# Attention scores one step later in three head groups, probabilities turned in one step and weighed in the next, the last weight block in two column halves, lambda's operations fourteen steps later

## The chip, the cores and the metric

The kernel runs on one core of one Trainium2 chip. The metric is the device time of one execution in microseconds (us). The profiled execution gives, beside its own time, a span: the stretch from the first to the last recorded instruction, which is what all positions below are counted in. A core has a matrix engine (TensorE, PE in the profile, with PEld for its weight loads), a vector engine (DVE), a scalar engine (ACT), a general engine (POOL) and a sync engine (SP) that here only issues transfers. Each engine works through its own list of instructions in order, and engines wait for one another by semaphores. SP, ACT and POOL can issue transfers (DMA) from their lists.

## The reference

Two layers over a sequence of 256 rows of width 2048, all in float32. Layer 0 mixes with a state-space scan, layer 1 with differential attention, and each is followed by a SwiGLU network of width 5632. Every part is normed before and after:

```python
for i in range(DEPTH):                       # DEPTH = 2
    h = rmsnorm(x, norm_mix_pre[i])
    m = ssd_mixer(h, ...) if i % 2 == 0 else diff_attention(h, ...)
    x = x + rmsnorm(m, norm_mix_post[i])
    h = rmsnorm(x, norm_ffn_pre[i])
    x = x + rmsnorm(swiglu(h, ...), norm_ffn_post[i])

def diff_attention(...):                     # 16 heads, 2 maps of width 64, v of width 128
    lam = exp(sum(lq1 * lk1)) - exp(sum(lq2 * lk2)) + lambda_init
    # per block of 128 queries, causal:
    pr = softmax(s)                          # s: scores of both maps
    pr = pr[:, :, 0] - lam * pr[:, :, 1]
    o = pr @ v                               # per head
    o = rmsnorm(o, subln_w) * (1 - lambda_init)
    return o @ w_out
```

## The kernel before, in words

**Products.** The matrix engine keeps float32 accuracy by splitting each operand in a high and a low part: ACT casts the high part `hi` (L137), DVE subtracts to get the low part `lo` (L138), and a product is three matmuls, hi by hi, hi by lo and lo by hi. Weights come in blocks of 1 MB, sent by SP's queue into three raw buffers; each block is split in two passes of 128x2048 and used by halves. The 256 rows of x are two tiles, `t` = 0 and 1. `mv` (L181) holds x as the stationary operand and streams 512 columns of weights: for each half block it runs the six matmuls of t = 0 at once and puts those of t = 1 on a list that is worked off a few halves later. When a tile's last half is through, it calls `evac` for the accumulated tile `acc`, which lies in one of four PSUM buffers. `ws` does the q and k products of the attention, with the weights stationary (L239, L241) and four column tiles `acc[0..3]`, which need all four PSUM buffers.

**What sets the order.** Small work is not written where it is needed but handed to `later(k, fn)`, which runs `fn` k steps on; a step (`tick`) is one half block of `mv` or `ws`, 12 matmuls of 512 columns in `mv`. The order of the code so made is then passed through a scheduler that sets the final order on each engine, so the code alone doesn't say what stands beside what.

**Attention.** `attention_group(hg)` handles four heads; there are four groups. It runs `mv` for v, `ws` for q and `ws` for k, and hands on, for the steps of the next group's `mv` and `ws`: `all_scores` (the scores of query tile 1 head pair 0, tile 0, tile 1 head pair 1, L1055, then the softmax operations on DVE and ACT), `turn` (transposes of the probabilities on the matrix engine, L1091, and their copy by ACT, L1093), `weigh` (probabilities by v, L1102, then a norm per head: square on ACT L1106, sums on DVE L1108 and L1109, a power on POOL L1111, a product on DVE L1112 into `ob`), and `piece` (transposes of `ob`, L326, for the output projection). The keys are scaled by `rstd_bc` on DVE (L1038) behind the addition L1035 that evacuates them; the scores wait for that. For the last group the steps are those of the output projection.

**Lambda.** `lamv`, a row of 256 numbers repeated over 128 partitions (128 KB on chip), is fetched by a DMA that ACT issues (L997). DVE multiplies and sums (L1000, L1001), ACT takes the exponent (L1002, with a load of its function table), DVE subtracts (L1004, L1005) into `neglam`, which the softmax uses. All this is written between the FFN of layer 0 and the first group. Between the two also lie the norms that end the FFN (`norm_chain`: x updated on DVE, L682, transposed on the matrix engine, L688 `ptx`, split into `xT`, L693 and L694).

**End.** `out_proj` accumulates the last FFN's output in four column blocks n of 512. On n = 3 the evacuation of each tile adds to `m` (L780), squares and sums on ACT (L337), multiplies by the norm's weights (L719, `mw`), and calls `norm_chain`, which here has `final` set: `rs_post` by L94 on DVE and L97 on POOL, then for n = 0 a scaling on ACT (L679) and an addition on POOL (L680), for n = 1 to 3 one operation on DVE (L682), and for each n a DMA of 256 KB to the output, all issued by SP (L684).

Of the kernel before, what the change touches and what calls it, by code (L numbers as in the profile page):

```python
# [45 lines left out]
def trunk_kernel(ctx, tc, x_rows, x_cols, vec_cols, vec64, post_rows, lam_rows,  # L46
# [134 lines left out]
    def mv(blocks, stat, evac, lag, scale=None, loaded=()):  # L181
# [3 lines left out]
        def run(i, t, hi, lo):  # L185
            if i == 0:
                acc[t] = accp.tile([P, 512], F32, tag="acc", name="acc")
            for j in range(2):
                xh, xl = stat(i, j, t)
                for q, (a, b) in enumerate(((xh, hi), (xh, lo), (xl, hi))):  # L190
                    nc.tensor.matmul(acc[t], a, b[:, j], start=(i == 0 and j == 0 and q == 0),  # L191
                                     stop=(i == last and j == 1 and q == 2))
            if i == last:
                evac(t, acc[t])
# [477 lines left out]
    def norm_chain(t, ss4, last_mw, step, final, t512):  # L672

        rn = rstd_of(ss4[:, 3:4], D, f"post{step}_{t}", ss4[:, 0:1])
        for n in range(4):
            mw = last_mw if n == 3 else m[(t, n)]
            xt = xres[(t, n)]
            if final and n == 0:
                nc.scalar.activation(mw, mw, AF.Copy, scale=rn)  # L679
                nc.gpsimd.tensor_tensor(xt, xt, mw, op=ALU.add)  # L680
            else:
                nc.vector.scalar_tensor_tensor(xt, mw, rn, xt, op0=ALU.mult, op1=ALU.add)  # L682
            if final:
                nc.sync.dma_start(out[t * P:(t + 1) * P, n * 512:(n + 1) * 512], xt)  # L684
                continue
# [23 lines left out]
    def out_proj(w, first, last, acts, kgs, step, final, lag, t512, pw, scale=None, ns=range(4), two={}, forms=None, md=None, mid=None,  # L709
# [56 lines left out]
        for n in ns:  # L766
# [7 lines left out]
            def evac(t, ps, n=n):  # L774
# [19 lines left out]
            if weave and n < 2:  # L794
# [5 lines left out]
               (lambda i: [scale[:, 2 * up[i] + j:2 * up[i] + j + 1] for j in range(2)]) if scale is not None else None)  # L800
# [195 lines left out]
    lamv = t512("lamv", (P, 4, 64))  # L996
    nc.scalar.dma_start(lamv, lam_rows.partition_broadcast(P))  # L997
    lsum = const.tile([P, 2], F32, name="lsum")
    for e in range(2):
        nc.vector.tensor_tensor(lamv[:, 2 * e], lamv[:, 2 * e], lamv[:, 2 * e + 1], op=ALU.mult)  # L1000
        nc.vector.tensor_reduce(lsum[:, e:e + 1], lamv[:, 2 * e], axis=AX.X, op=ALU.add)  # L1001
    nc.scalar.activation(lsum, lsum, AF.Exp)  # L1002
    neglam = const.tile([P, 1], F32, name="neglam")
    nc.vector.tensor_tensor(neglam, lsum[:, 1:2], lsum[:, 0:1], op=ALU.subtract)  # L1004
    nc.vector.tensor_scalar(neglam, neglam, -LAMBDA_INIT, None, op0=ALU.add)  # L1005
# [6 lines left out]
    def attention_group(hg):  # L1012
# [112 lines left out]
        later(2, all_scores)  # L1125
        later(6, lambda: turn(0, (0, 1)))
        later(8, lambda: (turn(1, (0,)), weigh(0)))
        later(10, lambda: turn(1, (1,)))
# [68 lines left out]
```

## Time and profile before

| what | value |
| --- | --- |
| median of three runs | 2509.29 us (2508.55, 2509.29, 2509.58) |
| profiled execution, its own time | 2509.47 us |
| span of that execution | 2507.6 us |
| granted clock of TensorE, mean | 0.999 |
| bytes moved | 541 MB, mean 216 GB/s |

The profiled execution lies 0.18 us above the median, and its span leaves 1.9 us of its time outside. A matmul's row gives its start and its length to the end of its drain; matmuls overlap, so that what one costs is the distance to the next one's start. In a row of the timeline the first number is the start, the second the length of the whole group, "x4" the number of instructions in it, and the bracket at the end says how long the engine was idle before and what released it.

### The profile page before, as it was taken

To read this page: it belongs to the slowest core of one execution; us is meant where nothing else is said; L and a number is where in the kernel's file an instruction comes from. 1 tells how busy PE (TensorE), PEld (TensorE's weight loads), DVE (VectorE), ACT (ScalarE), POOL (GpSimd) and SP (SyncE) were. 2 spreads that over 40 slices of the span, in tenths; PEclk is the share of its full clock that TensorE was granted. 3 is DMA by queue.
4 is the path that set the end of the run, shared out by engine and by line. 5 is a ranking of instruction groups with operands and counts; after the bars stand their busy time and mean duration, and the time that the engine had idled before them with its cause. 6 is when DMAs were issued, how large, how long until landed. Compare 5 with 4: busy or idle time off the path is not lost.

```text
span 2507.6 us, 31493 instructions
## 1 busy us (share of the span) xinstructions
PE 2489.6 (99%) x11818; PEld 2062.5 (82%) x11818; DVE 1936.8 (77%) x2394; ACT 1403.2 (56%) x1895; POOL 263.8 (11%) x242
## 2 busy tenths in 40 slices
PE   9999999999999999999999999999999999999998
PEld 8888888888888888888888888888888888888886
DVE  6877547777688899978987766556688899879985
ACT  5767546665565455545554654455655465546553
POOL 0131000121110010001001100001100100020002
PEclk9999999999999999999999999999999999999999
DMA  7555555555786786868676544544776967686774
GB/s 287 195 171 199 185 191 195 175 179 192 255 275 202 253 256 215 256 209 265 217 247 237 185 171 144 199 167 143 255 234 207 289 223 232 217 265 225 224 247 151
DMA packets 143385, 541.43 MB, mean 216 GB/s; under 512 B 14400, under 2 KB 31104, under 8 KB 116224
## 3 DMA queue, kind: packets, MB, share of 16 engines
q1 hardware_dynamic: 125872, 503.96, 57.7%
q0 software_dynamic: 16992, 35.13, 7.1%
q8 instruction: 93, 1.52, 0.2%
q14 instruction: 60, 0.49, 0.1%
q10 hardware_dynamic: 368, 0.32, 0.1%
HBM read 520.41 MB, written 18.94 MB: 215 GB/s over the span
## 4 chain that ended last, share of the span: by engine, by line
PE 93%; DVE 2%; issue 1%; ACT 1%; DMA 1%; POOL 0%; SPq 0%; DVEq 0%; ACTq 0%; POOLq 0%
PE acc L265 38%; PE acc L191 33%; PE cp L265 9%; PE acc L239 5%; PE acc L241 2%; PE acc L216 2%; DVE lo L138 1%; PE pt_f L326 1%; ACT hi L137 1%; DMA raw<-in_w_g_dram 1%; PE py L607 1%; PE ptx L688 0%; PE po L1102 0%; PE pc L509 0%; PE px L594 0%
## 5 line engine op out<-in xcount | busy, mean ns | idle before, releaser
L138 DVE TENSOR_TENSOR lo<-raw,hi 128x2048 fp32r<-128x2048 f32 (+2 forms) x401 | 728.8, 1821 | 307.8 <-ACT hi L137 300.9
L137 ACT CAST hi<-raw 128x2048 fp32r<-128x2048 f32 (+2 forms) x401 | 604.6, 1511 | 432.9 <-PE acc L191 122.7
L191 PE MATMUL acc<-hi,xT 128*128 128x512 f32 x1792 | 570.3, 394 | 0.0
L265 PE MATMUL acc<-hi,xT 128*128 128x512 f32 x1608 | 518.7, 390 | 0.1
L191 PEld LDWEIGHTS acc<-hi,xT 128*128 128x128 f32 x1792 | 336.0, 188 | 71.4 <-issue 2.2
L265 PEld LDWEIGHTS acc<-hi,xT 128*128 128x128 f32 x1608 | 301.8, 188 | 63.0 <-DVE sx L748 0.5
L191 PE MATMUL acc<-lo,xT 128*128 128x512 f32 x896 | 351.9, 393 | 1.4 <-DVE lo L138 1.4
L265 PE MATMUL acc<-lo,xT 128*128 128x512 f32 x804 | 313.0, 389 | 0.0
L138 DVE TENSOR_TENSOR lo<-rawm,hi 128x2048 fp32r<-128x2048 f32 (+1 forms) x87 | 181.8, 2089 | 35.0 <-ACT hi L137 33.7
L137 ACT CAST hi<-rawm 128x2048 fp32r<-128x2048 f32 (+1 forms) x87 | 152.7, 1755 | 95.6 <-PE acc L265 54.6
L191 PEld LDWEIGHTS acc<-lo,xT 128*128 128x128 f32 x896 | 168.4, 188 | 37.3 <-DVE lo L138 4.9
L239 PE MATMUL acc<-xT,hi 128*128 128x512 f32 x512 | 181.2, 399 | 0.0
L265 PEld LDWEIGHTS acc<-lo,xT 128*128 128x128 f32 x804 | 150.9, 188 | 31.2
L265 PE MATMUL acc<-hi,ah_f 128*128 128x512 f32 x450 | 176.1, 391 | 0.0
L265 PE MATMUL acc<-hi,al_f 128*128 128x512 f32 x450 | 175.2, 389 | 0.0
L265 PE MATMUL acc<-lo,ah_f 128*128 128x512 f32 x450 | 175.1, 389 | 0.0
L265 PE MATMUL cp<-sh,ff 128*128 128x512 f32 x516 | 172.8, 389 | 0.0
L241 PE MATMUL acc<-xT,lo 128*128 128x256 f32 x512 | 142.9, 280 | 0.0
L142 DVE SCALAR_TENSOR_TENSOR lo<-raw,cols,hi 128x512 fp32r<-128x512 f32 x128 | 93.5, 774 | 56.9 <-ACT hi L141 56.5
L141 ACT ACTIVATE hi<-raw,cols 128x512 fp32r<-128x512 f32 x128 | 84.7, 716 | 64.1 <-PE acc L191 42.2
L239 PEld LDWEIGHTS acc<-xT,hi 128*128 128x128 f32 x512 | 96.1, 188 | 22.7
L265 PEld LDWEIGHTS cp<-sh,ff 128*128 128x128 f32 x516 | 96.9, 188 | 20.1
(305 smaller groups left out, 4081.5 us busy)
## 6 DMA issues: line engine op xcount, KB each, us to landing
raw<-in_w_zxbc_dram SPq DMA_DIRECT2D x77, 1024.0 KB, 4.8
raw<-in_w_d_dram SPq DMA_DIRECT2D x98, 512.0 KB, 5.8
raw<-in_w_g_dram SPq DMA_DIRECT2D x96, 512.0 KB, 6.5
raw<-in_w_u_dram SPq DMA_DIRECT2D x96, 512.0 KB, 5.9
raw<-in_w_qkv_dram SPq DMA_DIRECT2D x48, 1024.0 KB, 4.8
raw<-in_w_so_dram SPq DMA_DIRECT2D x32, 1024.0 KB, 4.8
rawm<-in_w_g_dram SPq DMA_DIRECT2D x64, 512.0 KB, 5.9
rawm<-in_w_u_dram SPq DMA_DIRECT2D x64, 512.0 KB, 6.1
```

The costliest lines, as they stand in the source:

```text
L137: nc.scalar.copy(hi, raw)
L138: nc.vector.tensor_tensor(lo, raw, hi.bitcast(F32), op=ALU.subtract)
L141: nc.scalar.activation(hi[:, j], raw[:, j], AF.Copy, scale=scale[j])
L142: nc.vector.scalar_tensor_tensor(lo[:, j], raw[:, j], scale[j], hi[:, j].bitcast(F32), op0=ALU.mult, op1=ALU.subtract)
L191: nc.tensor.matmul(acc[t], a, b[:, j], start=(i == 0 and j == 0 and q == 0), stop=(i == last and j == 1 and q == 2))
L216: nc.tensor.matmul(acc[job, t], a, b[:, j], start=(i == 0 and j == 0 and q == 0), stop=(i == last and j == 1 and q == 2))
L239: nc.tensor.matmul(acc[ct], hi[:, j, cs], x.rearrange("p a s -> p (a s)"), start=(i == 0 and j == 0), stop=False)
L241: nc.tensor.matmul(acc[ct][:, :S], lo[:, j, cs], x[:, 0], start=False, stop=(i == last and j == 1))
L265: nc.tensor.matmul(acc[k], a, b, start=first and q == 0, stop=last and q == 2)
L326: nc.tensor.transpose(pt[:, j], src[:, j * P:(j + 1) * P], ident)
L607: nc.tensor.matmul(py[e * 64:(e + 1) * 64, a], xd[c][:, 2 * a + e], mts[c][:, 2 * a + e], start=True, stop=True)
```

## The change

Four parts, none of which alters what is computed.

1. In groups 0 to 2 `all_scores` runs three steps after the keys' product, before two (`k` is 1 there, 0 in the last group). The three `turn` operations, before at steps 6, 8 and 10, run together at step 9+k; the two `weigh`, before at 8 and 11, together at 10+k; the pieces, before at 13, at 12+k.
2. Lambda's DMA and operations go into a function that runs 14 steps later, inside the first group's products.
3. In the last block of columns of the last FFN (n = 3), the tile t = 1 closes its accumulation one half block early: that sum is evacuated, and the last half block is run in two halves of 256 columns into two fresh PSUM tiles, each evacuated by `halfway` (addition, square and sum, weights).
4. In the final `norm_chain`, n = 0 is done by the same DVE operation as the others, n = 3 in two halves, and the output's DMAs are issued by SP and ACT in turn: ACT has n = 1 and the first half of n = 3.

```diff
@@ -178,19 +178,28 @@
             pending.popleft()()
 
 
-    def mv(blocks, stat, evac, lag, scale=None, loaded=()):
+    def mv(blocks, stat, evac, lag, scale=None, loaded=(), cut=False):
         acc = {}
         last = 2 * len(blocks) - 1
 
         def run(i, t, hi, lo):
             if i == 0:
                 acc[t] = accp.tile([P, 512], F32, tag="acc", name="acc")
-            for j in range(2):
-                xh, xl = stat(i, j, t)
-                for q, (a, b) in enumerate(((xh, hi), (xh, lo), (xl, hi))):
-                    nc.tensor.matmul(acc[t], a, b[:, j], start=(i == 0 and j == 0 and q == 0),
-                                     stop=(i == last and j == 1 and q == 2))
-            if i == last:
+            end = cut and i == last and t == 1
+            if end:
+                evac(t, acc[t])
+            for cs in (slice(0, 256), slice(256, 512)) if end else (slice(0, 512),):
+                if end:
+                    acc[t] = accp.tile([P, 512], F32, tag="acc", name="acc")
+                for j in range(2):
+                    xh, xl = stat(i, j, t)
+                    for q, (a, b) in enumerate(((xh, hi), (xh, lo), (xl, hi))):
+                        nc.tensor.matmul(acc[t][:, cs], a, b[:, j, cs],
+                                         start=((i == 0 or end) and j == 0 and q == 0),
+                                         stop=(i == last - (cut and t == 1 and not end) and j == 1 and q == 2))
+                if end:
+                    evac(t, acc[t], cs)
+            if i == last and not end:
                 evac(t, acc[t])
 
         for b, src in enumerate(blocks):
@@ -675,13 +684,12 @@
         for n in range(4):
             mw = last_mw if n == 3 else m[(t, n)]
             xt = xres[(t, n)]
-            if final and n == 0:
-                nc.scalar.activation(mw, mw, AF.Copy, scale=rn)
-                nc.gpsimd.tensor_tensor(xt, xt, mw, op=ALU.add)
-            else:
-                nc.vector.scalar_tensor_tensor(xt, mw, rn, xt, op0=ALU.mult, op1=ALU.add)
+            for cs in (slice(0, 256), slice(256, 512)) if final and n == 3 else (slice(0, 512),):
+                nc.vector.scalar_tensor_tensor(xt[:, cs], mw[:, cs], rn, xt[:, cs], op0=ALU.mult, op1=ALU.add)
+                if final:
+                    (nc.scalar if n % 2 and not cs.start else nc.sync).dma_start(
+                        out[t * P:(t + 1) * P, n * 512 + cs.start:n * 512 + cs.stop], xt[:, cs])
             if final:
-                nc.sync.dma_start(out[t * P:(t + 1) * P, n * 512:(n + 1) * 512], xt)
                 continue
             pt = aux("ptx")
             for j in range(4):
@@ -771,7 +779,29 @@
                 else:
                     pw(n)
 
-            def evac(t, ps, n=n):
+            def halfway(t, ps, cs):
+                mt = m[(t, 3)]
+                nc.vector.tensor_tensor(mt[:, cs], mt[:, cs], ps[:, cs], op=ALU.add)
+                if cs.start == 0:
+                    last_mw.append(t512("mw"))
+                    sa = small.tile([P, 1], F32, tag="ss1", name="ssh", bufs=3)
+                else:
+                    sa = ss4[t][:, 3:4]
+                row_sumsq(sa, mt[:, cs], t512("junk")[:, cs])
+                if cs.start == 0:
+                    nc.vector.scalar_tensor_tensor(ss4[t][:, 0:1], sa, 1.0 / D, ss4[t][:, 0:1], op0=ALU.mult, op1=ALU.add)
+                nc.vector.tensor_tensor(last_mw[0][:, cs], mt[:, cs], pw(3)[:, cs], op=ALU.mult)
+                if cs.start:
+                    norm_chain(t, ss4[t], last_mw[0], step, final, t512)
+
+            last_mw = []
+
+            def evac(t, ps, cs=None, n=n):
+                if cs is not None:
+                    return halfway(t, ps, cs)
+                if final and n == 3 and t == 1:
+                    nc.vector.tensor_tensor(m[(t, n)], m[(t, n)], ps, op=ALU.add)
+                    return
                 if first:
                     if n == 0:
                         m_tile(t)
@@ -797,7 +827,8 @@
                     mvs(woven, [(0, 0), (0, 1), (0, 2), (1, 0), (1, 1), (1, 2), (0, 3), (1, 3)], up_stat, lag)
                 continue
             mv([w[n, kg // 2] for kg in up[::2]], up_stat, evac, LAG if last and n == 3 else lag,
-               (lambda i: [scale[:, 2 * up[i] + j:2 * up[i] + j + 1] for j in range(2)]) if scale is not None else None)
+               (lambda i: [scale[:, 2 * up[i] + j:2 * up[i] + j + 1] for j in range(2)]) if scale is not None else None,
+               cut=final and n == 3)
 
     for half in range(2):
         if half == 0:
@@ -993,16 +1024,20 @@
 
     causal = t512("causal", (P, P))
     make_causal_mask(nc, causal, NEG)
-    lamv = t512("lamv", (P, 4, 64))
-    nc.scalar.dma_start(lamv, lam_rows.partition_broadcast(P))
     lsum = const.tile([P, 2], F32, name="lsum")
-    for e in range(2):
-        nc.vector.tensor_tensor(lamv[:, 2 * e], lamv[:, 2 * e], lamv[:, 2 * e + 1], op=ALU.mult)
-        nc.vector.tensor_reduce(lsum[:, e:e + 1], lamv[:, 2 * e], axis=AX.X, op=ALU.add)
-    nc.scalar.activation(lsum, lsum, AF.Exp)
     neglam = const.tile([P, 1], F32, name="neglam")
-    nc.vector.tensor_tensor(neglam, lsum[:, 1:2], lsum[:, 0:1], op=ALU.subtract)
-    nc.vector.tensor_scalar(neglam, neglam, -LAMBDA_INIT, None, op0=ALU.add)
+
+    def lam():
+        lamv = t512("lamv", (P, 4, 64))
+        nc.scalar.dma_start(lamv, lam_rows.partition_broadcast(P))
+        for e in range(2):
+            nc.vector.tensor_tensor(lamv[:, 2 * e], lamv[:, 2 * e], lamv[:, 2 * e + 1], op=ALU.mult)
+            nc.vector.tensor_reduce(lsum[:, e:e + 1], lamv[:, 2 * e], axis=AX.X, op=ALU.add)
+        nc.scalar.activation(lsum, lsum, AF.Exp)
+        nc.vector.tensor_tensor(neglam, lsum[:, 1:2], lsum[:, 0:1], op=ALU.subtract)
+        nc.vector.tensor_scalar(neglam, neglam, -LAMBDA_INIT, None, op0=ALU.add)
+
+    later(14, lam)
     subc = const.tile([P, 1], F32, name="subc")
     nc.vector.tensor_scalar(subc, subln, 1.0 - LAMBDA_INIT, None, op0=ALU.mult)
 
@@ -1122,12 +1157,11 @@
             for x in (a, b, c):
                 softmax(*x)
 
-        later(2, all_scores)
-        later(6, lambda: turn(0, (0, 1)))
-        later(8, lambda: (turn(1, (0,)), weigh(0)))
-        later(10, lambda: turn(1, (1,)))
-        later(11, lambda: weigh(1))
-        later(13, lambda: (piece(0), piece(1)))
+        k = hg < 3
+        later(2 + k, all_scores)
+        later(9 + k, lambda: (turn(0, (0, 1)), turn(1, (0,)), turn(1, (1,))))
+        later(10 + k, lambda: (weigh(0), weigh(1)))
+        later(12 + k, lambda: (piece(0), piece(1)))
 
     for hg in range(4):
         attention_group(hg)
```

How the order on the engines changes, at the three places that matter below. First the matrix engine at the scores of the first group; `acc<-hi` and `acc<-lo` are matmuls of the next group's `mv`, `xT` its stationary operand, `sc` the scores. Before:

```order
L191 MATMUL acc<-lo_12087,xT_99 128x512
L191 MATMUL acc<-hi_12086,xT_99 128x512
L1055 MATMUL sc_12103<-qk 128x256
L1055 MATMUL sc_12104<-qk 128x256
L1055 MATMUL sc_12103<-qk 128x256
```

And after:

```order
L197 MATMUL acc<-hi_12086,xT_99 128x512
L197 MATMUL acc<-hi_12105,xT_100 128x512
L197 MATMUL acc<-lo_12106,xT_100 128x512
L197 MATMUL acc<-hi_12105,xT_100 128x512 x2
L197 MATMUL acc<-lo_12106,xT_100 128x512
L197 MATMUL acc<-hi_12105,xT_100 128x512
L197 MATMUL acc<-hi_12086,xT_99 128x512
L197 MATMUL acc<-lo_12087,xT_99 128x512
L197 MATMUL acc<-hi_12086,xT_99 128x512 x2
L197 MATMUL acc<-lo_12087,xT_99 128x512
L197 MATMUL acc<-hi_12086,xT_99 128x512
L1090 MATMUL sc_12122<-qk 128x256
```

The first row after is the last row of `acc` before. Twelve matmuls of 512 columns, one step of `mv` (six on `xT_100`, six on `xT_99`), now stand between it and the scores. In the last group the scores' place is as before.

Next ACT between the FFN of layer 0 and the first group: `xT` are the split parts of x, `v` the evacuation of the first group's v, `lsum` lambda's exponent, `hi` the casts of the weights. Before:

```order
L693 ACTIVATE xT_101<-ptx,cols 128x128
L137 CAST hi_11635<-raw 128x2048
L693 ACTIVATE xT_102<-ptx,cols 128x128
L1002 ACT_TABLE_LOAD
L1002 ACTIVATE lsum<-lsum 128x2
L693 ACTIVATE xT_102<-ptx,cols 128x128
L337 ACTIVATE junk,ss_m<-m 128x512
L137 CAST hi_11666<-raw 128x2048
```

And after:

```order
L137 CAST hi_11745<-raw 128x2048
L701 ACTIVATE xT_101<-ptx,cols 128x128
L701 ACTIVATE xT_102<-ptx,cols 128x128
L1054 ACTIVATE v<-acc,rs_pre_0_11622 128x512
L1032 DMA lamv<-in_lam_rows_dram 128x256
L137 CAST hi_11783<-raw 128x2048
L137 CAST hi_11821<-raw 128x2048
L1036 ACT_TABLE_LOAD
L1036 ACTIVATE lsum<-lsum 128x2
L1054 ACTIVATE v<-acc,rs_pre_1_11700 128x512
```

The DMA of `lamv` now stands behind the first evacuation of v and the exponent ahead of the second; on DVE lambda's two products now stand right ahead of the subtraction that makes the low part of `hi_11783`, and its two sums right behind it.

Last, DVE at the end of the program; `m_19540` holds the output tile t = 1, `mw` its last columns by the norm's weights, `x` the output. Before:

```order
L780 TENSOR_TENSOR m_19540<-m_19540,acc_19978 128x512
L719 TENSOR_TENSOR mw_20072<-m_19540,wpost_19908 128x512
L94 TENSOR_SCALAR ms_post3_1_20074<-ss_m_19829 128x1
L682 SCALAR_TENSOR_TENSOR x_19771<-m_19540,rs_post3_1_20076,x_19771 128x512
L682 SCALAR_TENSOR_TENSOR x_19773<-m_19540,rs_post3_1_20076,x_19773 128x512
L682 SCALAR_TENSOR_TENSOR x_19773<-mw_20072,rs_post3_1_20076,x_19773 128x512
```

And after:

```order
L803 TENSOR_TENSOR m_19540<-m_19540,acc_19978 128x512
L784 TENSOR_TENSOR m_19540<-m_19540,acc_20065 128x256
L793 TENSOR_TENSOR mw_20073<-m_19540,wpost_19908 128x256
L784 TENSOR_TENSOR m_19540<-m_19540,acc_20079 128x256
L792 SCALAR_TENSOR_TENSOR ss_m_19829<-ssh_20074,ss_m_19829 128x1
L793 TENSOR_TENSOR mw_20073<-m_19540,wpost_19908 128x256
L94 TENSOR_SCALAR ms_post3_1_20090<-ss_m_19829 128x1
L688 SCALAR_TENSOR_TENSOR x_19771<-m_19540,rs_post3_1_20092,x_19771 128x512 x2
L688 SCALAR_TENSOR_TENSOR x_19773<-m_19540,rs_post3_1_20092,x_19773 128x512
L688 SCALAR_TENSOR_TENSOR x_19773<-mw_20073,rs_post3_1_20092,x_19773 128x256 x2
```

The full addition stands ahead of the last two quarter tiles, the addition behind the last matmul has 256 columns, and DVE has five operations on x behind `ms_post` where it had three; ACT's two scalings and POOL's two additions at this place are gone.

## The prediction

> **What bounds the kernel.** I read the page first, for who is busy and who is on the chain that ends last; then the waits of the matrix engine; then the timeline at each place that the change touches. From the page, the busy line and the chain by engine:
>
> ```profile
> PE 2489.6 (99%) x11818; PEld 2062.5 (82%) x11818; DVE 1936.8 (77%) x2394; ACT 1403.2 (56%) x1895; POOL 263.8 (11%) x242
> PE 93%; DVE 2%; issue 1%; ACT 1%; DMA 1%; POOL 0%; SPq 0%; DVEq 0%; ACTq 0%; POOLq 0%
> ```
>
> PE is busy 2489.6 of 2507.6 us. The change removes no matmul, so it can win only from the 18.0 us in which PE is not busy, plus the little that a restart costs. From the waits of PE (what waited, for what; us in total, times, longest):
>
> ```profile
> PE sc L1055 <- DVE qk L1038: 2.8, 4, 0.7
> PE ptx L688 <- DVE x L682: 1.5, 3, 0.7
> PE acc L191 <- DVE lo L138: 1.4, 4, 0.5
> ```
>
> The first line is the largest: the scores, in all four groups. The second and third lie at the norms, partly where lambda's work stands. The rest of the 18 us is mostly the start and the end of the program.
>
> **Scores one step later.** The timeline of PE, then of DVE, at the first group's scores:
>
> ```profile
> 1471.51 1.80 PE L1055 MATMUL sc<-qk 64*128 64x256 f32 x20
> 1474.01 1.36 PE L1055 MATMUL sc<-qk 64*128 64x128 f32 x12 [0.70 <-DVE qk L1038]
> 1475.64 0.39 PE L191 MATMUL acc<-lo,xT 128*128 128x512 f32 x1
> 1475.87 0.62 PE L191 MATMUL acc<-hi,xT 128*128 128x512 f32 x2
> ...
> 1470.67 2.29 DVE L138 TENSOR_TENSOR lo<-raw,hi 128x2048 fp32r<-128x2048 f32 x1 [1.03 <-ACT hi L137]
> 1472.88 0.41 DVE L1035 TENSOR_TENSOR qk<-qk,acc 128x256 f32<-128x256 f32 x1
> 1473.54 0.41 DVE L1038 TENSOR_TENSOR qk<-qk,rstd_bc 128x256 f32<-128x256 f32 x1
> ```
>
> Twenty score matmuls run, then PE stands still for 0.70 us until the last part of the keys is scaled; that operation ends at 1473.95 because it and its addition stand behind a subtraction of 2.29 us. The restart costs a little more: a matmul's length is longer than the distance to the next one's start (0.39 against 0.23 in the L191 rows), and in an unbroken row this 0.16 is hidden. So each stop costs 0.86. The change puts twelve matmuls of 512 columns ahead, 12 x 0.23 = 2.7 us: the part that waits would be reached at about 1476, the keys are ready at 1473.95. The wait goes with 2.7 − 0.7 = 2.0 us to spare, and the first score, reached at 1474.2, is past the keys too. The matmuls put ahead are those that follow the scores today, and their weights are split in time: the subtraction at 1470.67 is the second behind the one they need. Three groups: 3 x 0.86 = **−2.6**. The fourth keeps its place and its stop: 0. Bounds: −2.6 if all go, 0 if another operand of the moved matmuls is late by as much.
>
> **Turns together, weighs together, pieces.** The timeline of PE at a turn, the chain of one weigh with its norm, and the one wait of a piece (group four):
>
> ```profile
> 1486.32 0.60 PE L1091 MATMUL pp<-ident,e 128*128 128x128 f32 x4
> 1486.99 0.40 PE L191 MATMUL acc<-lo,xT 128*128 128x512 f32 x1
> ...
> 1505.26 1.95 PE L1102 MATMUL po<-v,prT 128*128 128x128 f32 x16
> ...
> 1507.24 0.60 ACT L1106 ACTIVATE ob<-po 128x512 f32<-128x512 f32 x1 [2.77 <-PE po L1102]
> 1507.87 0.69 DVE L1108 TENSOR_REDUCE sso<-ob 128x4 f32<-128x512 f32 x1 [1.56 <-ACT ob L1106]
> 1508.84 1.01 POOL L1111 TENSOR_TENSOR ro<-sso,mhalf 128x4 f32<-128x4 f32 x1 [10.19 <-DVE sso L1109]
> 1509.88 0.69 DVE L1112 TENSOR_TENSOR ob<-po,ro 128x512 f32<-128x512 f32 x1 [1.12 <-PE acc L239]
> 1735.37 0.66 PE L326 MATMUL pt_o<-ident,ob 128*128 128x128 f32 x4 [0.31 <-DVE ob L1112]
> ```
>
> Four transposes and one 512-column matmul between them and the second row take 0.67, so a transpose is (0.67 − 0.23)/4 = 0.11 and switching to them costs nothing that shows: running twelve of them together saves nothing. What the merge changes is slack. From the start of the second weigh to its `ob` takes 1509.88 + 0.69 − 1505.26 = 5.3. When both weighs run in one step, the pieces come two steps of about 2.8 later: from the first weigh's start, 1.0 (8 matmuls by half of 1.95) + 1.95 + 5.6 = 8.5 us. The second weigh's `ob` is then due at 1.0 + 5.3 + 1.0 (the second power behind the first on POOL) = 7.3. That leaves 1.2 us of slack, which covers the merge; a subtraction of 2.29 that gets in between would use it up and cost 1.1. I take 0 for three groups. In group four the distance from weigh to pieces shrinks for tile 0 only, and the stop of 0.31 (0.47 with the restart) stays; bounds 0 to +1.0 (both pieces waiting), −0.5 if it goes. I take 0, by that row.
>
> **Lambda fourteen steps later.** Lambda's operations, the evacuations of v, the landing of `lamv`, the windows that show the traffic (us, busy time of PE, PEld, DVE, ACT, POOL, clock, DMA share, GB/s), and PE at the fourth column tile of q:
>
> ```profile
> 1400.80 1.28 ACT L1002 ACT_TABLE_LOAD   x1
> 1402.10 0.20 ACT L1002 ACTIVATE lsum<-lsum 128x2 f32<-128x2 f32 x1
> 1414.98 0.77 ACT L1019 ACTIVATE v<-acc,rs_pre 128x512 f32<-128x512 f32 x1
> 1416.05 4.05 ACT L137 CAST hi<-raw 128x2048 fp32r<-128x2048 f32 x2
> 1423.68 0.69 ACT L1019 ACTIVATE v<-acc,rs_pre 128x512 f32<-128x512 f32 x1 [0.87 <-PE acc L191]
> ...
> 1397.78 0.35 DVE L1000 TENSOR_TENSOR lamv<-lamv 128x64 f32<-128x64 f32 x2
> 1398.05 0.34 DVE L1001 TENSOR_REDUCE lsum<-lamv 128x1 f32<-128x64 f32 x2
> ...
> DMA to landing us min/median/max: 5.3/5.3/5.3
> ...
> 1389.00:1395.00 6.00, 5.39 (x33) 4.35 (x32) 5.22 (x12) 4.01 (x8) 0.56 (x1) 1.00 0.81 312
> 1415.00:1420.00 5.00, 5.00 (x23) 4.14 (x23) 3.19 (x8) 4.88 (x6) 1.18 (x2) 1.00 0.00 0
> ...
> 1425.84 0.28 PE L241 MATMUL acc<-xT,lo 128*128 128x256 f32 x1
> 1425.95 0.39 PE L239 MATMUL acc<-xT,hi 128*128 128x512 f32 x1
> ```
>
> Taken from the old place: 1.5 us of ACT, about 1.0 of DVE. Two of the four waits for `lo` stand there; with restarts they cost 0.9 at most. In the new order the subtraction behind the first still follows an addition that waits for PE, and the transposes `ptx` stand two matmuls earlier, so that their wait for x takes over from the second: 0, bounds −0.9 to 0. At the new place the DMA stands on ACT's queue behind the first evacuation of v, which one cast of 2.0 now precedes: issued near 1414.98 + 2.0 + 0.77 ≈ 1417.7. Behind its landing come, in the order of the queues, the products 0.35, a subtraction 2.25, the sums 0.35, the exponent 0.20 and the second evacuation of v 0.69, about 3.9 (the table load stands ahead and runs while ACT waits). That evacuation frees the PSUM buffer of the fourth column tile, which PE wants at 1425.95. So the landing may take 1425.95 − 1417.7 − 3.9 ≈ 4.3 us. The only landing of `lamv` took 5.3, but with the DMA engines busy at a share of 0.81; near 1417 their share is 0.00. The output transfers below, twice as large, land in 2.0 when alone. I take 3.5: hidden, **0**, with the subtractions and casts queued behind it later by some 1.5 us and their matmuls two half blocks away. At 5.3 it costs +1.0: bounds 0 to +1.0.
>
> The load shows 1.28 us, and the exponent starts 0.02 behind its end. The Trainium skill (ScalarE: Activation LUTs, What ACT_TABLE_LOAD costs) puts 1380 ns of drain beside a load of 1283 ns, 2.66 us for a switch. The load's length agrees with the trace, the drain doesn't show. By the page's figure the exponent would hold the evacuation and PE by up to some 0.8, an estimate from that page, and the sum would be −3.1; I go by the row.
>
> **The end.** DVE, ACT and POOL behind the last matmul, the output's landing times, and the last issue of SP:
>
> ```profile
> 2498.09 0.69 DVE L780 TENSOR_TENSOR m<-m,acc 128x512 f32<-128x512 f32 x1 [1.32 <-PE acc L191]
> 2498.87 0.63 ACT L337 ACTIVATE junk<-m 128x512 f32<-128x512 f32 x1 [4.48 <-DVE m L780]
> 2499.92 0.54 POOL L97 TENSOR_TENSOR rs_post<-ms_post,mhalf 128x1 f32<-128x1 f32 x1 [3.70 <-DVE ms_post L94]
> 2500.50 1.42 DVE L682 SCALAR_TENSOR_TENSOR x<-m,rs_post,x 128x512 f32<-128x512 f32 x2 [0.66 <-POOL rs_post L97]
> 2501.30 1.74 POOL L680 TENSOR_TENSOR x<-x,m 128x512 f32<-128x512 f32 x1 [0.83 <-ACT m L679]
> 2501.83 1.75 DVE L682 SCALAR_TENSOR_TENSOR x<-mw,rs_post,x 128x512 f32<-128x512 f32 x1
> DMA to landing us min/median/max: 2.0/2.1/2.4
> 2503.96 0.40 SPq L684 DMA_DIRECT2D out_dram<-x  x1
> ```
>
> Here nothing hides anything. Four terms. The last half block in halves: a 256-column matmul is 0.11 to 0.12 from the next one (1425.84 to 1425.95), 12 x 0.12 against 6 x 0.23: +0.05. The addition has 256 columns: 0.41 (the row of L1035) for 0.69, −0.28; the square I shorten by 0.2, less than the addition. So `rs_post` is ready 0.4 earlier. From there, before, the last operation on x runs beside POOL's addition and takes 1.75 where the ones alone take 0.71, and the last DMA is issued 2503.96 − 2500.46 = 3.5 later; after, three operations of 0.71 and two of 0.41 end at 2.95, issue at 3.0: −0.5. The last three transfers, issued at 2503.06 (when POOL's addition ends) to 2503.96, queue on one another, so the last takes the 2.4; after, they are issued 0.4 to 0.7 apart, the last two half as large: 2.0, −0.4. Sum 0.4 + 0.5 + 0.4 = **−1.3**; bounds −0.8 (the landing stays, square no shorter) and −1.8 (the smaller transfers land 0.3 sooner, and ACT's queue takes more of the issuing).
>
> **Sum.** −2.6 + 0 + 0 − 1.3 = −3.9 on 2509.47, 2505.57. The profiled execution lies 0.18 above the median, so 2505.4. That is −0.16%. Some 0.2%, 5.0 us, is what a measurement of this kernel can tell from no change: below 2504.3 is faster, above 2514.3 slower.
>
> **The rivals.**
> - *More.* The two waits for `lo` at the norms go with lambda (−0.9), and the end reaches −1.8: 2504.0. For it: 2.5 us of work leaves two queues there. Against: the order still holds the first subtraction behind PE.
> - *Lambda lands late.* At 5.3, or with an exponent that starts later than the row says, PE waits 0.6 to 1.0 for the fourth tile: 2506.0 to 2506.4.
> - *The scores' wait moves.* The keys are in time, but the moved matmuls wait for a `lo` or a cast instead, 0.9 per group: only the end gains, 2508.0. Against: 2.0 us to spare.
> - *Slower.* The norm of the second weigh misses the pieces in groups one to three. If the casts (2.0) and subtractions (2.29) get between its five operations, the chain grows past the slack of 1.2; one more subtraction gives 3 x 1.1 = +3.3 and 2508.7. It decides the sign at 1.3 per group, and 2514.3 needs 3.0 per group, two subtractions too many.
>
> **How the numbers follow.** The case of the sum 0.62, its own range 2504.6 to 2506.2 from the bounds of the end and a lambda that is late by half. More: 0.17, about all of it at or beyond the faster bound; another 0.03 of the case of the sum lies there. Lambda late 0.09. The wait moves 0.08. Slower 0.04. So faster 0.20, same 0.76, slower 0.04. The range 2503.5 to 2507.5 takes in the first three with half a us beyond the fast end and one beyond a late lambda; outside are the wait that moves and the slower case.
>
> **What the profile will show.** Right, if the waits of PE have sc once at 0.7 instead of four times, no new line for the fourth column tile of q near 1426 or for pt_o in groups one to three, one pt_o wait of 0.3 in group four, and the last output issued about 0.9 earlier against the last matmul. Wrong, if a wait of `acc` for `hi` or `lo` stands where the scores waited, if `lamv` lands more than 4.3 us after its issue, or if `ob` comes behind PE's arrival at the pieces.

## The result, and the profile after

The changed kernel takes 2504.33 us (median of 15 runs, 2503.60 to 2504.76) against 2509.56 us for the kernel before on the same chips (15 runs, 2508.55 to 2510.01): ratio 0.9979, 95% interval 0.9973 to 0.9986, or −5.2 us. Forecast were 2505.4 us and −3.9 us, in a range from 2503.5 to 2507.5. The time lies in the range and within 0.1 us of the 2504.3 below which the prediction spoke of "faster"; its sum was 1.3 us short. The span fell from 2507.6 to 2503.0 us.

The waits of PE after (what waited, for what; us in total, times, longest):

```profile
PE ptx L696 <- DVE x L688: 1.8, 4, 0.7
PE acc L197 <- DVE lo L138: 0.9, 3, 0.3
PE sc L1090 <- DVE qk L1073: 0.7, 1, 0.7
```

The scores wait once, in the fourth group, instead of four times. One wait for a low part went, one of the transposes for x came. No line has the pieces (`pt_o`) any more. In the first group the timeline of PE, then of DVE, reads:

```profile
1474.17 0.39 PE L197 MATMUL acc<-hi,xT 128*128 128x512 f32 x1
1474.49 2.89 PE L1090 MATMUL sc<-qk 64*128 64x256 f32 x32
1477.31 0.50 PE L197 MATMUL acc<-hi,xT 128*128 128x512 f32 x1
...
1473.13 0.41 DVE L1070 TENSOR_TENSOR qk<-qk,acc 128x256 f32<-128x256 f32 x1
1473.58 0.43 DVE L1073 TENSOR_TENSOR qk<-qk,rstd_bc 128x256 f32<-128x256 f32 x1
```

All 32 score matmuls run in one piece: the keys are ready at 1474.01, before PE comes. From the first score to the next product are 1477.31 − 1474.49 = 2.82 us. In the kernel before the product behind the scores of this group has this row:

```profile
1475.30 0.50 PE L191 MATMUL acc<-hi,xT 128*128 128x512 f32 x1
```

There it was 1475.30 − 1471.51 = 3.79 us. A stop cost 0.97, not the 0.86 forecast.

At the end of the program, DVE, ACT, POOL, SP and the landing of the output:

```profile
2494.89 0.41 DVE L784 TENSOR_TENSOR m<-m,acc 128x256 f32<-128x256 f32 x1
2495.39 0.42 ACT L346 ACTIVATE junk<-m 128x256 f32<-128x256 f32 x1 [0.28 <-DVE ss_m L792]
2496.23 0.54 POOL L97 TENSOR_TENSOR rs_post<-ms_post,mhalf 128x1 f32<-128x1 f32 x1 [6.03 <-DVE ms_post L94]
2496.81 2.08 DVE L688 SCALAR_TENSOR_TENSOR x<-m,rs_post,x 128x512 f32<-128x512 f32 x3 [0.66 <-POOL rs_post L97]
2498.80 0.88 DVE L688 SCALAR_TENSOR_TENSOR x<-mw,rs_post,x 128x256 f32<-128x256 f32 x2
2499.70 0.33 SPq L690 DMA_DIRECT2D out_dram<-x  x1
DMA to landing us min/median/max: 2.0/2.1/2.3
```

From the last evacuation's start to `rs_post` 1.88 us pass (2.37 before), from there to the last issue 2.93 (3.50 before), and the last transfer lands sooner.

To compare runs I cut each span in stretches that begin and end with the same matmul: from the first transpose `ptx` near 1392 to the first near 1789, which holds the transition and all of the attention; from there to the last matmul's start; from that to the end of the span. The rest lies ahead of 1392, has the same code in all of these kernels, and ends between 1391.9 and 1393.2. In us, worked out from the matmuls' starts in each trace:

| kernel | attention | to the last matmul | behind it | median |
| --- | --- | --- | --- | --- |
| before | 397.35 | 708.10 | 9.94 | 2509.56 |
| changed | 393.34 | 708.49 | 8.57 | 2504.33 |
| only the scores | 393.84 | 708.01 | 9.95 | 2507.06 |
| only the merge | 396.18 | 708.19 | 9.94 | 2508.70 |
| only lambda | 396.98 | 707.97 | 10.88 | 2510.68 |
| only the end | 396.77 | 708.22 | 9.56 | 2509.07 |
| changed, fourth group too | 393.09 | 708.28 | 8.58 | 2504.51 |
| changed, outputs on SP | 393.50 | 708.00 | 8.57 | 2505.02 |
| changed, no halves | 393.03 | 707.98 | 9.00 | 2505.28 |

In "before" and "only the end" the code in the attention is the same, and the stretch differs by 0.6: differences below that in the first column say nothing by themselves. The 0.6 has a place. From the first to the last `acc<-xT,hi` of the q and k products of groups two to four, before takes 47.84, 47.83 and 47.85, and "only the end" 47.83, 47.53 and 47.55. With the same code a group takes 0.3 less in some traces; the runs don't say why.

The last column's medians, of 11 to 15 runs each, scatter by about half a us; before had 2509.39 to 2509.68 in the other comparisons. One run of the scores alone (5099.77 us) and one of the kernel before beside it (4198.59 us) were far slower than all others; they count in the medians, not in the ratios.

### The profile page after: what moved, and what is told of

Its sections match the earlier page's. It is cut to its first block, busy times and chain, and to the rows that moved or that the text cites. A ratio compares the mean times of both kernels' runs of the same rounds, so it can differ in the third digit from the quotient of the medians.

```text
span 2503.0 us, 31504 instructions
## 1 busy us (share of the span) xinstructions
PE 2488.6 (99%) x11824; PEld 2063.0 (82%) x11824; DVE 1937.0 (77%) x2402; ACT 1402.4 (56%) x1895; POOL 260.1 (10%) x240
## 4 chain that ended last, share of the span: by engine, by line
PE 94%; DVE 2%; DMA 2%; issue 1%; ACT 1%; POOL 0%; SPq 0%; DVEq 0%; POOLq 0%; ACTq 0%
PE acc L274 37%; PE acc L197 33%; PE cp L274 9%; PE acc L248 5%; PE acc L250 2%; PE acc L225 2%; DMA raw<-in_w_g_dram 1%; DVE lo L138 1%; PE pt_f L335 1%; PE py L616 1%; ACT hi L137 1%; PE ptx L696 0%; PE pc L518 0%; PE po L1137 0%; PE sc L1090 0%
## 5 line engine op out<-in xcount | busy, mean ns | idle before, releaser
L307 DVE TENSOR_TENSOR sl<-raw,sh 128x1536 fp32r<-128x1536 f32 x54 | 94.9, 1757 | 24.0 <-ACT sh L304 21.5
```

The source lines that it names most:

```text
L307: nc.vector.tensor_tensor(sl[:, 0:3], raw[:, 0:3], sh[:, 0:3].bitcast(F32), op=ALU.subtract)
```

## The experiments

**Each part alone.** First the scores:

```diff
-        later(2, all_scores)
+        later(2 + (hg < 3), all_scores)
```

> Only the scores of groups 0 to 2 a step later; turns, weighs, pieces, lambda and the end as before. Theory (each part's saving stands alone; the scores' stop is worth what the changed kernel's trace shows, 0.91 of idle and 0.15 of restart per group): 3 x 1.06 = -3.2 us, and the waits of PE show the scores' wait for the keys once instead of four times. Rival (the later scores need the later turns: the first turn, still at step 6, now waits for its probabilities, which come 2.0 to 2.7 us later and had 3.8 us of slack less the 0.9 that PE gains): a new wait of a turn of 0.3 to 1.3 us per group, so -2.3 to +0.7 us.

Measured: 2507.06 us, −2.4 (ratio 0.9990, 0.9980 to 0.9999). The attention is 397.35 − 393.84 = 3.5 shorter. Two of its groups have the q and k products 0.3 shorter (47.55 and 47.53), which leaves 2.9, three times 0.97. PE's waits:

```profile
PE sc L1055 <- DVE qk L1038: 0.7, 1, 0.7
PE pt_o L326 <- DVE ob L1112: 0.3, 1, 0.3
```

Three of four stops are gone and no turn waits: the rival fell. The later scores do not need the later turns.

Then the merge, with the scores at step 2:

```diff
-        later(6, lambda: turn(0, (0, 1)))
-        later(8, lambda: (turn(1, (0,)), weigh(0)))
-        later(10, lambda: turn(1, (1,)))
-        later(11, lambda: weigh(1))
-        later(13, lambda: (piece(0), piece(1)))
+        k = hg < 3
+        later(9 + k, lambda: (turn(0, (0, 1)), turn(1, (0,)), turn(1, (1,))))
+        later(10 + k, lambda: (weigh(0), weigh(1)))
+        later(12 + k, lambda: (piece(0), piece(1)))
```

> Only the turns together (step 9, in groups 0 to 2 step 10) and the weighs together a step later, pieces at 12 or 13; scores, lambda and the end as before. Theory (the merge frees the fourth group's wait of the pieces for ob, 0.47 us with the restart, and nothing else): -0.5 us, all four scores' waits of 0.7 still there. Rival 1 (the prediction's term): 0. Rival 2 (fewer changes between kinds of matmul save PE time in each group): -1 us or more.

Measured: 2508.70 us, −0.8 (0.9998, 0.9989 to 1.0007: no difference by the interval). In its trace the scores wait four times as before, and the fourth group's pieces run in one row:

```profile
PE sc L1055 <- DVE qk L1038: 2.8, 4, 0.8
...
1733.79 1.10 PE L326 MATMUL pt_o<-ident,ob 128*128 128x128 f32 x8
```

The prediction's 0 for the fourth group is off; its stop goes with the merge. Compared matmul by matmul with before, the trace gains 0.46 at these pieces. Of the 1.2 by which its attention is shorter, 0.4 lie in the q and k products; whether the switching saves the rest can't be told at this size, and the 1 us or more of the second rival isn't there.

Lambda alone has the edit of the change (part 2).

> Only lambda's operations 14 steps later. Theory (one wait for a low part goes, a wait of the transposes for x takes its place, as the changed kernel's trace shows): 0, within 0.3 us; the landing of lamv about 3.1 us, no wait of the fourth column tile. Rival (the work taken from the norms was holding PE): -0.9 us, with both waits for a low part gone.

Measured: 2510.68 us, +1.2 (1.0003, 0.9994 to 1.0012). The attention is within the scatter of before (396.98): behind the norms its only difference from before beyond 0.1 us is one of 0.3 in a group's q and k products. The time was lost where this kernel's code is that of before: behind the last matmul, 10.88 us against 9.94. The landing times of its output:

```profile
DMA to landing us min/median/max: 2.0/2.1/3.3
```

The end alone has parts 3 and 4 of the change.

> Only the end: the last half block in two column halves, n = 0 on DVE, outputs issued by SP and ACT. Theory: -1.4 us, all of it behind the last matmul (from the last matmul's start to the span's end 8.6 us, before 9.9). Rival (the parts of the change help one another, or the medians' difference of 5.2 us against 4.6 in the spans has its place here): -1.9 us or more.

Measured: 2509.07 us, −0.4 (0.9998, 0.9989 to 1.0007). Behind the last matmul 9.56 us, not the 8.57 of the changed kernel, though every step to the last issue is the same to 0.01 us. The transfers of this kernel from 2500 to 2507 and of the changed kernel from 2497 to 2503 (what was moved in 40 slices, and the queues):

```profile
GB/s 0 0 0 0 0 0 0 0 0 246 386 421 386 305 386 398 398 387 386 433 340 340 351 351 340 47 23 23 23 23 23 23 0 0 0 0 0 0 0 0
q14 instruction: 1, 0.01, 0.8%
out_dram<-x SPq DMA_DIRECT2D x1, 128.0 KB, 3.1
...
GB/s 0 0 0 0 0 0 0 0 0 150 423 396 423 328 328 423 437 382 342 437 382 423 389 335 403 355 403 226 7 0 0 0 0 0 0 0 0 0 0 0
out_dram<-x SPq DMA_DIRECT2D x1, 128.0 KB, 2.1
```

In the run of the end alone a block of 8 KB of instructions is fetched in this window, and behind the 390 GB/s follow 1.0 us at 23 GB/s, about a sixteenth: as if one of the sixteen engines were still at its share when the others are done. The kernel ends with the last part. In the changed kernel this fetch came after the span's end.

**Is it the fetch?** 32 copies of one column on ACT and 32 on DVE, in the attention, are put in to move the fetches. They write into a new tile, `pad`.

```diff
+    pad = const.tile([P, 2], F32, name="pad")
...
             es[t] = ob
+            for _ in range(4):
+                nc.scalar.copy(pad[:, 0:1], ob[:, 0, 0:1])
+            for _ in range(4):
+                nc.vector.tensor_copy(pad[:, 1:2], ob[:, 0, 0:1])
```

> The end alone as in the run before of it, and 32 copies of one column each on ACT and on DVE, spread over the attention behind the norm of each weigh, where both engines have gaps; nothing waits for them. They move the place at which the two engines' instruction streams cross a block of 8 KB. Theory (in the run of the end alone an 8 KB transfer of the instruction queue fell among the last output transfers and held one of their sixteen parts up by 1 us): the stretch from the last matmul's start to the span's end falls from 9.56 to 8.6 us, and the median lies 1.4 below before instead of 0.4 (up to 0.3 less if the copies get in the way). Rival (the landing is late because of the way the outputs are issued): 9.5 us again, -0.4.

> Lambda alone 14 steps later, with the same 32 copies on ACT and on DVE. Theory (the 1.2 us that lambda alone cost were the late fetch of instructions at the end, not lambda): the stretch behind the last matmul's start falls from 10.88 to 9.94 us as in the kernel before, the median lies within 0.4 of before. Rival (lambda at the new place costs time in the first group): +0.7 to +1.2 again.

Measured: the end alone 2539.61 us, lambda alone 2540.76, both 30 us slower, which neither the theory nor a rival had. The stretch behind the last matmul answers the question all the same: 8.66 with the end (9.56 without the copies), 10.05 with lambda (10.88), and the last fetches of 8 KB now lie near 2486, ahead of the outputs. The third of this kind put the new tile and six copies on ACT into the changed kernel, to bring a fetch into the outputs:

```diff
             es[t] = ob
+            if hg == 0:
+                for _ in range(3):
+                    nc.scalar.copy(pad[:, 0:1], ob[:, 0, 0:1])
```

> The changed kernel with six copies of one column on ACT behind the norms of the first group, nothing else moved. ACT then has as many instructions, within one, as in the run of the end alone. Theory (the block of instructions that is fetched last belongs to ACT, and six instructions bring its fetch from behind the end into the output transfers): the stretch behind the last matmul's start grows from 8.57 to about 9.5 us, the median to -4.2 against before (from -5.2). Rival (the place of the fetch isn't set by ACT's count, or the fetch is not what holds the transfer): 8.6 us, -5.2.

Measured: 2535.49 us, and 8.67 behind the last matmul: this one missed. The last fetch moved ahead of the outputs instead of among them; which engine's count sets it the runs don't tell.

**The 30 us.** Two runs part the copies from the tile. The copies into a tile that is there:

```diff
             es[t] = ob
+            for _ in range(4):
+                nc.scalar.copy(lsum[:, 0:1], ob[:, 0, 0:1])
+                nc.vector.tensor_copy(lsum[:, 1:2], ob[:, 0, 0:1])
```

> The end alone and the 32 copies on ACT and DVE, this time into a tile that is there already and no longer read (lambda's sums), so that no tile's place on the chip changes. Theory (the end is worth 1.4 us where no fetch of instructions meets the outputs, and the 30 us of the run before came from the new tile of 8 bytes per partition): -1.4 us against before, the stretch behind the last matmul's start 8.6 us. Rival (the copies themselves cost the 30 us): 2539 us again.

and the tile without copies, in the changed kernel:

```diff
+    pad = const.tile([P, 2], F32, name="pad")
+    nc.gpsimd.memset(pad, 0.0)
```

> The changed kernel with one more constant tile of 8 bytes per partition, written once at the start and never read; no copies. Theory (the tile moves those behind it, and the matmuls with x stationary then follow one another at 0.234 us instead of 0.227): 2535 us, 30 above the changed kernel. Rival (the copies cost the 30 us): 2504 us.

Measured: the tile alone 2535.61 us (1.0104, 1.0089 to 1.0120), the copies alone 2509.54 (1.0001, 0.9992 to 1.0010). So the tile costs the 30 us; the six copies above had it too, at 2535.49. Two groups of matmuls, first in the changed kernel, then with the tile (ns, least, median, most):

```profile
L197 PE MATMUL acc<-hi,xT x1792: 387/389/505, 7.4 to 1838.8; 128*128 128x512 f32 x200
L197 PE MATMUL acc<-hi,ah_f x130: 277/389/478, 1352.4 to 2494.2; 128*128 128x512 f32 x126, 128*128 128x256 f32 x4
...
L197 PE MATMUL acc<-hi,xT x1792: 388/396/504, 7.4 to 1860.8; 128*128 128x512 f32 x200
L197 PE MATMUL acc<-hi,ah_f x130: 278/389/478, 1372.0 to 2525.1; 128*128 128x512 f32 x126, 128*128 128x256 f32 x4
```

The matmuls on `xT` take 7 ns more each and follow one another at 234 ns instead of 227 (median distances of the starts); those on `ah_f` don't change. Summed over all matmuls of 512 columns with `xT` stationary, the longer distances make 31.7 us, which is all of it: the spans differ by 31.0.

The run with copies into the old tile had 8.57 behind the last matmul, as the theory wants for the end, and no 8 KB fetch behind 2457, but not the −1.4 in its median. Its attention is 1.0 longer than that of before (398.32 against 397.35). One wait in the output projection, with its restart, makes up the difference: three of the copies stand ahead of a cast on ACT there, and the cast ahead of the `ah_o` that PE needs.

```profile
PE acc L225 <- ACT ah_o L341: 0.7, 1, 0.7
```

**The end in parts, and the fourth group.** All outputs issued by SP:

```diff
-                    (nc.scalar if n % 2 and not cs.start else nc.sync).dma_start(
+                    nc.sync.dma_start(
```

> The changed kernel with all output transfers issued by SP. The last half of the last column block is then issued behind three others on one queue, each 0.33 to 0.4 us. Theory: the operations on x end 0.4 apart at the last, so SP keeps up to within 0.3 us: +0.1 to +0.4 us against the changed kernel. Rival (issuing from two engines is what brings the landing forward): +0.8 us or more.

Measured: 2505.02 us; 8.57 behind the last matmul, as in the changed kernel. The last issue comes 0.14 later (3.07 behind `rs_post`, from 2.93) and the rest is 0.14 shorter. By the stretch, issuing from two engines is worth nothing here, and the rival fell. The median's 0.7 above the changed kernel lies in no stretch that the edit touches.

No column halves:

```diff
-                if final and n == 3 and t == 1:
-                    nc.vector.tensor_tensor(m[(t, n)], m[(t, n)], ps, op=ALU.add)
-                    return
...
-               cut=final and n == 3)
```

> The changed kernel without the two column halves of the last half block: the last evacuation has 512 columns again, the DVE operations on x and the issue by SP and ACT stay as changed. Theory (the prediction's terms): the reciprocal root of the last tile comes 0.4 us later, the rest as in the changed kernel: +0.4 us in the stretch behind the last matmul. Rival (the halves also bring the outputs' landing forward): +0.8 us or more; rival 2 (twelve matmuls of 256 columns cost more than the shorter evacuation wins): 0 or below.

Measured: 2505.28 us; 9.00 behind the last matmul, +0.43, all between the last matmul and `rs_post` (2.80 against 2.36). That is the theory's term.

The scores a step later in the fourth group too:

```diff
-        later(2 + k, all_scores)
+        later(3, all_scores)
```

> The changed kernel with the scores a step later in the fourth group too; turns, weighs and pieces of that group as in the change (steps 9, 10, 12). Theory: the last wait of the scores for the keys (0.91 and 0.15 of restart) goes: -1.06 against the changed kernel, so -6.3 against before. Rival (the fourth group's steps are shorter of slack, since its pieces feed the products that run beside it): a new wait of the first turn or of the pieces takes it back, -5.2 or less.

Measured: 2504.51 us, −5.2 as the changed kernel (0.9979, 0.9970 to 0.9988). The waits of PE, behind those of `ptx`:

```profile
PE acc L197 <- DVE lo L138: 1.3, 4, 0.5
PE acc L197 <- ACT hi L137: 0.7, 1, 0.7
```

The line of the scores is gone. The wait for `hi` that is new here stands at the start of the program (near 7 us), where the edit does nothing. PE at the fourth group's scores, first in the changed kernel, then here:

```profile
1696.01 1.80 PE L1090 MATMUL sc<-qk 64*128 64x256 f32 x20
1699.79 0.50 PE L225 MATMUL acc<-hi,ah_o 128*128 128x512 f32 x1
...
1699.71 2.89 PE L1090 MATMUL sc<-qk 64*128 64x256 f32 x32
1702.53 0.50 PE L225 MATMUL acc<-hi,ah_o 128*128 128x512 f32 x1
```

From the first score to the next product are 3.78 and 2.82: the stop's 0.96 is saved, as the theory has it. But the attention is only 0.25 shorter. Compared matmul by matmul, this trace loses 0.35 to the changed kernel between 1600 and 1620, in q and k products that the edit doesn't touch, and 0.24 near 1716.5, where two matmuls of the output projection start late; what held these I did not find. Whether this version is faster can't be told by its median. No version was clearly faster than the changed kernel.

## Why the prediction was right, and where its terms were off

**Scores: right, a tenth small.** The mechanism, the three groups, the fourth unchanged and the margin are in the trace: the keys ready at 1474.01, the scores started at 1474.49. The stop cost 0.97 by the rows in place of 0.86; the part alone gave 2.9 at the scores where −2.6 was forecast. The term that was mis-sized is the restart: the prediction priced it by the drain of a 512-column matmul (0.16, from the L191 rows), and the rows give 0.27 beside the idle 0.70.

**Merge: groups one to three right, the fourth wrong.** The prediction let "the stop of 0.31 (0.47 with the restart)" stay because it counted steps and not time; that it goes was only its bound of −0.5. Before, the second weigh of that group and the pieces stood as follows (PE before):

```profile
1729.93 1.95 PE L1102 MATMUL po<-v,prT 128*128 128x128 f32 x16
1734.46 0.60 PE L326 MATMUL pt_o<-ident,ob 128*128 128x128 f32 x4
```

4.5 us from the weigh's start to the pieces, where the prediction's own chain takes 5.3. Between them stand twelve matmuls of 512 columns, one step and not the two of the step numbers: by the code the output projection asks for the pieces (`lookup`) before their own step comes. After, PE, then DVE:

```profile
1723.05 2.84 PE L1137 MATMUL po<-v,prT 128*128 128x128 f32 x24
1731.18 1.11 PE L335 MATMUL pt_o<-ident,ob 128*128 128x128 f32 x8
...
1725.18 2.29 DVE L138 TENSOR_TENSOR lo<-raw,hi 128x2048 fp32r<-128x2048 f32 x1 [4.46 <-ACT hi L137]
1727.38 1.27 DVE L1143 TENSOR_REDUCE sso<-ob 128x4 f32<-128x512 f32 x2
1730.89 0.69 DVE L1147 TENSOR_TENSOR ob<-po,ro 128x512 f32<-128x512 f32 x1 [0.28 <-POOL ro L1146]
```

Now 24 matmuls stand between. The second weigh begins about 0.9 behind 1723.05, so 7.2 us are left to the first piece; the stop of 0.47 goes. It goes by luck: a subtraction of 2.29 got between here, as the slower rival feared for the other groups, and the second `ob` is ready at 1731.58, when PE reaches the transposes that need it at 1731.63. In groups one to three no subtraction gets between. The second `ob` is ready 1.2 ahead of the pieces, which is the slack that was forecast, and the slower rival did not come.

**Lambda: right.** ACT after, then DVE, the landing and PE at the fourth column tile:

```profile
1417.16 0.34 ACTq L1032 DMA_DIRECT2D lamv<-in_lam_rows_dram  x1
1423.10 1.28 ACT L1036 ACT_TABLE_LOAD   x1
1424.39 0.20 ACT L1036 ACTIVATE lsum<-lsum 128x2 f32<-128x2 f32 x1
1424.50 0.67 ACT L1054 ACTIVATE v<-acc,rs_pre 128x512 f32<-128x512 f32 x1
...
1420.27 0.36 DVE L1034 TENSOR_TENSOR lamv<-lamv 128x64 f32<-128x64 f32 x2 [0.44 <-DMA lamv<-in_lam_rows_dram]
...
DMA to landing us min/median/max: 3.1/3.1/3.1
...
1426.21 0.39 PE L248 MATMUL acc<-xT,hi 128*128 128x512 f32 x1
```

The landing took 3.1 (taken 3.5, limit 4.3); DVE stood 0.44 for it, and the evacuation of v ended at 1425.17, 1.0 before PE needed the buffer. The table load stands behind a cast and ahead of the exponent, which starts 0.01 behind it. The figure of 1380 ns of drain that the Trainium skill gives (ScalarE: Activation LUTs, What ACT_TABLE_LOAD costs) does not appear in this trace either; with it, by an estimate from that page, the evacuation would have ended near 1426.55 and the buffer been 0.3 late. The trade at the norms came as forecast, one wait for a low part kept, the other replaced by one for x:

```profile
1404.83 0.50 PE L197 MATMUL acc<-lo,xT 128*128 128x512 f32 x1 [0.27 <-DVE lo L138]
1408.95 0.66 PE L696 MATMUL ptx<-ident,x 128*128 128x128 f32 x4 [0.22 <-DVE x L688]
```

**The end: right in size and parts, by one piece of luck.** Forecast −0.4, −0.5 and −0.4; measured behind the last matmul −0.44 to `rs_post`, −0.57 to the last issue, −0.36 to the end: −1.37 against −1.3. What the prediction did not see is that the landing also depends on where a fetch of instructions falls: the same edit alone gained 0.4.

**The sum.** Three stops 2.9, the fourth group's pieces 0.47 and the end 1.37 make 4.7, and the span fell by 4.6. Part of that agreement is chance, since stretches with the same code moved too: the one ahead of the attention and the one behind it by +0.4 each, a group's q and k products by −0.3. The medians differ by 5.2. The profiled run of the changed kernel, 2504.76, is the slowest of its 15, which would explain 0.4 of the difference; that is not shown further.

The measured 2504.33 lies below the range that the prediction gave to the case of its sum, 2504.6 to 2506.2 (the bounds it names there would make 2504.9 to 2506.4). Of the 1.3 that its sum was short, the restarts (0.3) and the fourth group's pieces (0.5) make 0.8. The rival "more" named the right size for other reasons: its two waits at the norms did not both go, and the end did not reach −1.8. The chance of 0.04 for slower does not follow from that rival's price: at 2508.7 it would still have counted as the same.

## What to carry to other kernels

A wait repeated in each group is worth its idle time and its restart: read it as the distance between the work before it and the work behind it, in a group with the wait and one without. When small work is moved by steps, work out the time between producer and consumer, not the number of steps, and look whether the consumer waits for its own step at all. And time each part of a change alone, with the stretches of the span compared one by one: here two parts looked worthless or harmful by their medians because of a microsecond at the end that has nothing to do with what either part was made for.

## What the runs showed of the hardware

An 8 KB fetch of instructions that fell among the last output transfers went with about 1.0 us of delay: 23 GB/s at the end in place of nothing, the last landing in 3.1 to 3.3 us in place of 2.1 to 2.5. That it is the fetch rests on two kernels with it and the delay and on the same two with the fetch moved and no delay, one of them also without the new tile. All fourteen traces agree: only in these two does a fetch start while an output transfer is still more than 0.2 us from its landing, and only in these two does any output take more than 2.5 us. The six copies that should have brought the fetch back moved it elsewhere. How it delays the transfer is open: its own packet took 0.89 us in the end alone and only 0.31 with lambda alone, for the same delay.

One more constant tile of 8 bytes per partition, never read, slowed the kernel by 31 us: the matmuls with `xT` as stationary operand went from one per 227 ns to one per 234 ns, those with `ah_f` stayed at 227. That the tile does this by moving the tiles behind it is argued and not shown, and by which rule the runs don't tell.
